# The gate-weight tile and the compressed-probability step of a sparse-attention layer, moved

## The chip, the cores and the metric

The kernel runs on one core of a Trainium2 chip. The metric is the device time of one execution in microseconds (us). A core has five engines with a queue each: PE (matrix multiply), DVE (vector), ACT (scalar functions and copies), POOL (general) and SP, which here only starts DMAs. Each queue is worked off in order; engines wait for each other through semaphores. PE writes into PSUM, and the others move data from there to SBUF, the on-chip memory from which PE reads. PE's weight loads stand apart in the profile as PEld.

## The reference, cut to what matters

Two layers over 256 positions of width 1024: the first with latent attention, the second with sparse attention, each followed by a layer of looked-up experts (PEER). The change lies in the second layer's attention. Each of 16 heads (4 groups of 4) sees three branches: compressed blocks of 32 keys, selected blocks, and a window. At this size the last two reduce to causal attention over all positions, with keys and values of their own. The three results are added with gates that are sigmoids of a projection.

```python
proj = x @ w_in
q = proj[..., :B_HEADS * B_DK]
q_rot = rope(q)
gates = jax.nn.sigmoid(proj[..., B_HEADS * B_DK:])
...
p_c = masked_softmax(qb . k_cmp * scale, cmp_end <= t)
o_c = p_c . v_cmp
...
p_s = masked_softmax(qrb . k_g * scale, tok <= t)
o_s = p_s . v_g
...
p_w = masked_softmax(qrb . k_w * scale, m_w)
o_w = p_w . v_w
return gate0 * o_c + gate1 * o_s + gate2 * o_w
```

## The kernel before

All weights come as one stream of 512 KB tiles, in the order of the list in `plan()`. SP loads a tile into one of four raw places; ACT casts it to `hi` (L173), and a vector engine writes the rest to `lo` (L187); PE multiplies hi and lo parts of weights and activations (L267), three products for each. A raw place comes free when the tile four ahead has its `lo`. `nxt()` hands out the next tile: it emits the casts of the tiles two or three ahead, and then calls `tick()`. A tick counts up and runs what `defer(n, f)` put off for n ticks. So the order of each engine's queue is the order in which Python emits, and a tile that is moved moves the ticks with it.

In `nsa()` the order of work before is:

- Four tiles `s_wT` give the keys and values to be compressed (`kk`). POOL adds position vectors to them (`fm`).
- One tile `b_wg` holds the gate weights (48 of 128 columns are used). Its projection goes through ACT's sigmoid (L1495) to `gs`.
- Four more tiles `s_wT` give the keys of the two rotated branches, two tiles each. `rope_T` (L1345) multiplies on DVE (`ropeU`, `ropeV`) and combines on POOL (`ropeO`). It turns the layout through memory: a DMA writes `bounce`, and another reads it into `kr`. For the first branch both DMAs go through SP, a tick and two ticks later; for the second through POOL, at once. Five ticks later `k_split` splits `kr` with three ACT operations and a DVE one (L1510 to L1513) into `ks` and `klo`. After the second branch PE transposes `gs` (L294), and DVE copies it to `gates` (L1508).
- Eight tiles `b_wq` give the queries. A group of four heads takes two tiles, and each group goes through `rope_T` and `q_split` (L1524, L1525) to `qs`. The unrotated query is copied by ACT to `qu` (L1550). Between the first four query tiles stand four steps of `compress`, which multiply `fm` with the first layer of the compression network. Its hidden values `hb` go through ACT's Gelu, its second layer to the compressed keys `kcp` and values `vcp`.
- A loop of 19 steps over the heads. In step st PE makes the scores of head st (`ks`, `klo` with `qs`), DVE their maxima `m` (L1692, L1693), and ACT the exponentials `p` (L1716, L1719). DVE, or DVE and POOL, normalises `p` of head st-1 with the gates (L1729). PE transposes `p` of head st-2, ACT copies it to `pT` (L1710), and every second step PE sums the values of a pair of heads. The compressed branch goes in two halves of eight heads beside it: `cmp_scores` (`kcp` with `qu`, DVE L1634), `cmp_exp`, `cmp_sum` (POOL L1651) and `cmp_T`. The last has PE transpose `pc` (L294) and ACT copy it to `pcT` (L1657). For the first half these stand at the ends of steps 1, 2, 3 and 4, for the second at 5, 6, 7 and 9.

The ACT functions sigmoid, Gelu and exponential need tables; `ACT_TABLE_LOAD` changes them, and `warm()` (L307) changes them ahead of use with a small activation.

Of the kernel before, what the change touches and what calls it, by code (L numbers as in the profile page):

```python
# [18 lines left out]
AF = mybir.ActivationFunctionType  # L19
# [28 lines left out]
class Kern:  # L48
# [5 lines left out]
    def plan(self):  # L54
# [10 lines left out]
        for l in (0, 1):  # L65
            if l == 1 and "nsa" in self.parts:
                L += [I["s_wv"][i] for i in range(4)]
                L += [I["s_wT"][i] for i in range(4)]
                L += [I["b_wg"]]
                L += [I["s_wT"][i] for i in range(4, 8)]  # L70
                L += [I["b_wq"][i] for i in range(4)]
                L += [I["b_wq"][i] for i in range(4, 8)]
                L += [I["b_wo"][i] for i in range(KC)] + [I["b_wo"][i] for i in range(KC // 2)]
# [1332 lines left out]
    def nsa(self, hN, gb):  # L1406
# [4 lines left out]
        with es:  # L1411
# [79 lines left out]
            hi, lo = self.nxt()  # L1491
            gp = self.ps()
            self.proj_T(gp[:, 0:S], hi, lo, xhi, xlo, KC)
            gs = tmp.tile([48, S], F32, tag="gs", name="gs", bufs=1)
            nc.scalar.activation(gs, gp[0:48, 0:S], AF.Sigmoid)  # L1495

            for br in range(2):
# [6 lines left out]
                if br == 1:  # L1504
                    gt = self.ps()
                    for tt in range(2):
                        self.tr(gt[:, tt * 48:tt * 48 + 48], gs[:, tt * P:(tt + 1) * P])
                    nc.vector.tensor_copy(gates, gt[:, 0:96].rearrange("p (a b) -> p a b", a=2))  # L1508
# [60 lines left out]
            self.warm(AF.Gelu)  # L1569
            hp = self.acc(1)  # L1570
            turn = [0, 0]
            self.vlim = self.si + 7
            for step in "qqcc", "qc", "qc":
                for x in step:
                    if x == "q":
# [93 lines left out]
            for half, when in ((0, (1, 2, 3, 4)), (1, (5, 6, 7, 9))):  # L1669
# [3 lines left out]
            for st in range(NH + 3):  # L1673
# [49 lines left out]
                if 0 <= h < NH:  # L1723
# [3 lines left out]
                    for br, eng in ((1, nc.gpsimd if 4 <= h < NH - 2 else nc.vector), (0, nc.vector)):  # L1727
                        for tt, c in enumerate((slice(0, P), slice(P, 384))):
                            eng.tensor_scalar(p[:, br, c], p[:, br, c], m[:, 3, 2 * tt + br:2 * tt + br + 1],  # L1729
                                              gates[:, tt, 16 * br + 16 + h:16 * br + 17 + h], op0=OP.mult, op1=OP.mult)  # L1730
                h = next((h for h in range(1, NH, 2) if h + (4 if h < 6 else 3) == st), None)
                if h is not None:
# [4 lines left out]
                    for e in range(2):  # L1737
                        self.mm(o[e], vcp[:, hb, (h - 1 + e) % 8, :], pcT[:, hb, :], True, False)
                    for br in range(2):
                        c = br * 256 + g * 64  # L1740
                        for e in range(2):
                            self.mm(o[e], vN[:, 0, c:c + 64], pp[e][:, br, 0:S], False, False)
                        for e in range(2):
                            self.mm(o[e][:, P:S], vN[:, 1, c:c + 64], pp[e][:, br, S:384], False, br == 1)
# [114 lines left out]
```

## Time and profile before

| | before |
|---|---|
| median of 3 runs | 1579.82 us (1579.65 to 1583.05) |
| the profiled execution | 1585.52 us |
| its span, first to last instruction | 1583.5 us |
| matmul clock granted, mean | 0.996 of full |
| stage of the change: first compressed tile to the end of the head loop | about 782 to 907 us of the span |
| PE busy, 800 to 814 | 14.00 of 14 us |
| PE busy, 814 to 830 | 13.93 of 16 us |
| PE busy, 830 to 855 | 21.82 of 25 us |
| DVE busy, 830 to 855 | 22.56 of 25 us |
| PE busy, 880 to 906 | 25.50 of 26 us |

A time in a row of the timeline is counted from the start of the span. Busy times are of one execution. PE's matmuls are pipelined and their ends are modelled, so its starts are more reliable than its ends. A row names the engine, the line, the operation, what is written and what is read, the shapes and a count; in brackets stands the idle time ahead of it and what ended it.

### The profile page before, as it was taken

To read this page: it belongs to the slowest core of one execution; us is meant where nothing else is said; L and a number is where in the kernel's file an instruction comes from. 1 tells how busy PE (TensorE), PEld (TensorE's weight loads), DVE (VectorE), ACT (ScalarE), POOL (GpSimd) and SP (SyncE) were. 2 spreads that over 40 slices of the span, in tenths; PEclk is the share of its full clock that TensorE was granted. 3 is DMA by queue.
4 is the path that set the end of the run, shared out by engine and by line. 5 is a ranking of instruction groups with operands and counts; after the bars stand their busy time and mean duration, and the time that the engine had idled before them with its cause. 6 is when DMAs were issued, how large, how long until landed. Compare 5 with 4: busy or idle time off the path is not lost.

```text
span 1583.5 us, 27544 instructions
## 1 busy us (share of the span) xinstructions
PE 1551.1 (98%) x10018; PEld 1395.6 (88%) x10018; DVE 1387.3 (88%) x3218; ACT 680.8 (43%) x1351; POOL 535.3 (34%) x458
## 2 busy tenths in 40 slices
PE   7999999999999999999998999999999999999997
PEld 6879999999998888888887789999999988888886
DVE  5778889999969999999778789899999869999998
ACT  6665201212225555556367854111121245555553
POOL 2010134443325434431353210344443436434420
PEclk9999999999999999999999999999999999999999
DMA  7626899999999999999564257999999999999992
GB/s 240 202 84 225 330 409 408 408 408 371 396 381 371 373 366 347 357 368 322 187 228 149 79 195 279 408 409 408 408 407 362 371 372 406 353 368 344 360 356 92
DMA packets 140215, 511.03 MB, mean 323 GB/s; under 512 B 14160, under 2 KB 16752, under 8 KB 138992
## 3 DMA queue, kind: packets, MB, share of 16 engines
q1 hardware_dynamic: 89712, 324.70, 55.2%
q0 software_dynamic: 50368, 184.57, 30.6%
q8 instruction: 79, 1.29, 0.3%
q14 instruction: 56, 0.46, 0.1%
HBM read 503.45 MB, written 5.24 MB: 321 GB/s over the span
## 4 chain that ended last, share of the span: by engine, by line
PE 77%; DVE 11%; DMA 8%; ACT 2%; issue 2%; POOL 1%; SPq 0%; ACTq 0%; POOLq 0%; DVEq 0%
PE acc L267 44%; PE mm L267 32%; DMA row<-p_ur,xidx 4%; DVE row L584 3%; DMA nat<-p_u 1%; PE mm L294 1%; DVE lo L187 1%; DMA raw<-a_wv 1%; DVE hot L765 1%; DVE hot L776 1%; DMA raw<-s_wT 1%; DMA xT<-xT 1%; ACT hi L173 1%; DMA kr<-bounce 0%; DVE p L1729 0%
## 5 line engine op out<-in xcount | busy, mean ns | idle before, releaser
L267 PE MATMUL acc<-hi,W 128*128 128x512 f32 x1452 | 408.0, 389 | 0.0
L571 POOL DMA_INDIRECT row<-p_v,gidx x128 | 237.3, 1854 | 311.4 <-DVE gacc L608 243.8
L267 PE MATMUL mm<-xF,nat 128*128 128x160 f32 x2304 | 322.9, 300 | 1.4 <-DMA nat<-p_u 1.3
L267 PEld LDWEIGHTS acc<-hi,W 128*128 128x128 f32 x1452 | 272.5, 188 | 56.4
L267 PEld LDWEIGHTS mm<-xF,nat 128*128 128x128 f32 x2304 | 314.6, 190 | 2.7 <-issue 2.2
L267 PE MATMUL acc<-lo,W 128*128 128x512 f32 x968 | 298.1, 389 | 0.0
L187 DVE TENSOR_TENSOR lo<-raw,hi 128x1024 fp32r<-128x1024 f32 (+1 forms) x202 | 245.2, 1220 | 45.0 <-ACT hi L173 32.5
L173 ACT CAST hi<-raw 128x1024 fp32r<-128x1024 f32 (+1 forms) x207 | 215.1, 1046 | 153.1 <-PE acc L267 110.8
L571 POOL DMA_INDIRECT row<-p_ur,gidx x128 | 140.3, 1096 | 267.6 <-DVE row L584 167.1
L267 PEld LDWEIGHTS acc<-lo,W 128*128 128x128 f32 x968 | 181.8, 188 | 37.7
L173 ACT CAST hi<-spare 128x1024 fp32r<-128x1024 f32 x122 | 128.2, 1051 | 109.0 <-PE acc L267 107.1
L584 DVE SCALAR_TENSOR_TENSOR row<-row,gacc 128x1024 f32<-128x1024 f32 x128 | 155.6, 1218 | 6.5 <-DMA row<-p_ur,gidx 5.8
L608 DVE SCALAR_TENSOR_TENSOR gacc<-row,ggate,gacc 128x1024 f32<-128x1024 f32 x126 | 160.9, 1277 | 0.0
L187 DVE TENSOR_TENSOR lo<-spare,hi 128x1024 fp32r<-128x1024 f32 x122 | 148.7, 1218 | 10.7 <-ACT hi L173 10.7
L267 PE MATMUL mm<-xF,raw 128*128 128x160 f32 x896 | 125.8, 300 | 0.0
L267 PE MATMUL mm<-xF,more 128*128 128x160 f32 x896 | 125.7, 300 | 0.0
L267 PEld LDWEIGHTS mm<-xF,more 128*128 128x128 f32 x896 | 122.6, 190 | 0.0
L267 PEld LDWEIGHTS mm<-xF,raw 128*128 128x128 f32 x896 | 122.6, 190 | 0.0
L801 ACT ACTIVATE A<-acc 128x208 f32<-128x208 f32 (+19 forms) x116 | 37.4, 346 | 190.1 <-DVE A L799 163.4
L891 ACT ACTIVATE A<-mm 128x320 f32<-128x320 f32 (+13 forms) x104 | 38.3, 368 | 176.7 <-PE mm L267 175.0
L911 DVE TENSOR_TENSOR W<-A,W 128x128 fp32r<-128x128 f32 (+1 forms) x512 | 106.9, 249 | 0.0
L571 POOL DMA_INDIRECT row<-p_ur,xidx x64 | 66.0, 1032 | 104.6 <-DVE row L584 43.9
(308 smaller groups left out, 2074.5 us busy)
## 6 DMA issues: line engine op xcount, KB each, us to landing
nat<-p_u SPq DMA_DIRECT2D x144, 512.0 KB, 8.7
spare<-p_v SPq DMA_DIRECT2D x64, 1024.0 KB, 9.0
raw<-p_v SPq DMA_DIRECT2D x63, 1024.0 KB, 8.6
raw<-p_u SPq DMA_DIRECT2D x56, 512.0 KB, 16.3
more<-p_u SPq DMA_DIRECT2D x56, 512.0 KB, 18.3
raw<-p_wq SPq DMA_DIRECT2D x32, 512.0 KB, 4.3
raw<-b_wo SPq DMA_DIRECT2D x12, 512.0 KB, 4.1
raw<-a_wo SPq DMA_DIRECT2D x8, 512.0 KB, 3.5
```

Source lines behind the costliest of these rows:

```text
L173: self.nc.scalar.copy(self.his[i], self.raws[i])
L187: e.tensor_tensor(self.los[i], raw, self.his[i].bitcast(F32), op=OP.subtract)
L267: self.nc.tensor.matmul(out, a, b, start=start, stop=stop)
L294: self.nc.tensor.transpose(out, in_, self.ident[:n, :n])
L571: nc.gpsimd.indirect_dma_start(out=t, out_offset=None, in_=table, in_offset=bass.IndirectOffsetOnAxis(ap=at, axis=0))
L584: nc.vector.scalar_tensor_tensor(t, t, 1.0, x, op0=OP.mult, op1=OP.mult, accum_out=d[:, c:c + 1])
L608: nc.vector.scalar_tensor_tensor(gacc, t, ggate[:, c:c + 1], gacc, op0=OP.mult, op1=OP.add)
L765: tt(h[:, 0:2].rearrange("p w g i s -> p (w g) i s"), self.iota4[:, 0, None].to_broadcast([P, 4, P, 2]), selI[:, t0 // 4].rearrange("p w ( ...
L776: tt(o, oj, x[:, :, None, :].to_broadcast(b4), op=OP.mult)
L801: nc.scalar.activation(x[:, m:n, t0:t0 + 4], pv[:, j0 + m:j0 + n], AF.Copy, scale=sc_)
L891: nc.scalar.activation(y[:, :, n:NU], ps[:, :, n:NU], AF.Gelu)
L911: nc.vector.tensor_tensor(WW[j][:, o:o + c.stop - c.start], slot(j)[:, c], WW[j][:, c].bitcast(F32), op=OP.subtract)
```

## The change

Three things are moved; no arithmetic is added or removed.

1. In the stream the tile `b_wg` goes from ahead of the last four `s_wT` tiles to behind the first two query tiles. Its projection and the sigmoid become `gate_tile()`, the transposes of `gs` and the copy to `gates` become `gate_T()`, and the hand-written order of query tiles (q) and compress steps (c) becomes q q g c c t, q c, q c. The switch to the Gelu table moves into `gate_tile()`. The limit `vlim` on early loads counts one tile more, because one more tile is still to come.
2. The transposes of the first half's `pc` go from the end of step 4 into step 5, behind the transposes of `p`.
3. In the sums of all pairs of heads, the two matmuls with `pcT` go from first to last.

```diff
--- before.py
+++ after.py
@@ -66,10 +66,10 @@
             if l == 1 and "nsa" in self.parts:
                 L += [I["s_wv"][i] for i in range(4)]
                 L += [I["s_wT"][i] for i in range(4)]
+                L += [I["s_wT"][i] for i in range(4, 8)]
+                L += [I["b_wq"][i] for i in range(2)]
                 L += [I["b_wg"]]
-                L += [I["s_wT"][i] for i in range(4, 8)]
-                L += [I["b_wq"][i] for i in range(4)]
-                L += [I["b_wq"][i] for i in range(4, 8)]
+                L += [I["b_wq"][i] for i in range(2, 8)]
                 L += [I["b_wo"][i] for i in range(KC)] + [I["b_wo"][i] for i in range(KC // 2)]
             if f"peer{l}" in self.parts:
                 L += [I["p_wq"][l, i] for i in range(16)]
@@ -1488,11 +1488,20 @@
                     nc.gpsimd.tensor_tensor(f[:, 8:16, g, :], b, posT[:, i, 8:16, None].to_broadcast([P, 8, 15]), op=OP.add)
                 fm.append(f)
 
-            hi, lo = self.nxt()
-            gp = self.ps()
-            self.proj_T(gp[:, 0:S], hi, lo, xhi, xlo, KC)
             gs = tmp.tile([48, S], F32, tag="gs", name="gs", bufs=1)
-            nc.scalar.activation(gs, gp[0:48, 0:S], AF.Sigmoid)
+
+            def gate_tile():
+                hi, lo = self.nxt()
+                gp = self.ps()
+                self.proj_T(gp[:, 0:S], hi, lo, xhi, xlo, KC)
+                nc.scalar.activation(gs, gp[0:48, 0:S], AF.Sigmoid)
+                self.warm(AF.Gelu)
+
+            def gate_T():
+                gt = self.ps()
+                for tt in range(2):
+                    self.tr(gt[:, tt * 48:tt * 48 + 48], gs[:, tt * P:(tt + 1) * P])
+                nc.vector.tensor_copy(gates, gt[:, 0:96].rearrange("p (a b) -> p a b", a=2))
 
             for br in range(2):
                 ps = self.ps()
@@ -1501,11 +1510,6 @@
                     self.proj_T(ps[:, hf * S:(hf + 1) * S], hi, lo, xhi, xlo, KC)
                 kr = tmp.tile([64, G, S], F32, tag="raw4", name="kr")
                 self.rope_T(tmp, ps.rearrange("p (a t) -> p a t", a=2), rK, kr, 1, 2, br == 1)
-                if br == 1:
-                    gt = self.ps()
-                    for tt in range(2):
-                        self.tr(gt[:, tt * 48:tt * 48 + 48], gs[:, tt * P:(tt + 1) * P])
-                    nc.vector.tensor_copy(gates, gt[:, 0:96].rearrange("p (a b) -> p a b", a=2))
                 def k_split(br=br, kr=kr):
                     nc.scalar.copy(ks[0:64, :, br, :], kr)
                     nc.vector.tensor_tensor(klo[0:64, :, br, :], kr, ks[0:64, :, br, :].bitcast(F32), op=OP.subtract)
@@ -1566,12 +1570,14 @@
                                 w1[q][:, i, m % 4, :], m == 0, m == 15)
 
 
-            self.warm(AF.Gelu)
             hp = self.acc(1)
             turn = [0, 0]
-            self.vlim = self.si + 7
-            for step in "qqcc", "qc", "qc":
+            self.vlim = self.si + 8
+            for step in "qqgcct", "qc", "qc":
                 for x in step:
+                    if x in "gt":
+                        (gate_tile if x == "g" else gate_T)()
+                        continue
                     if x == "q":
                         q_tile(turn[0])
                         turn[0] += 1
@@ -1666,7 +1672,7 @@
                      4: ((7, 1), (7, 2))}
             beside = {2 * k + (7 if k < 3 else 6): lambda k=k: self.out_step(k) for k in range(KC - 2)}
             cmp_at = {}
-            for half, when in ((0, (1, 2, 3, 4)), (1, (5, 6, 7, 9))):
+            for half, when in ((0, (1, 2, 3, None)), (1, (5, 6, 7, 9))):
                 for w, f in zip(when, (cmp_scores, cmp_exp, cmp_sum, cmp_T)):
                     cmp_at[w] = lambda f=f, half=half: f(half)
             pr, pts = {}, {}
@@ -1728,20 +1734,22 @@
                         for tt, c in enumerate((slice(0, P), slice(P, 384))):
                             eng.tensor_scalar(p[:, br, c], p[:, br, c], m[:, 3, 2 * tt + br:2 * tt + br + 1],
                                               gates[:, tt, 16 * br + 16 + h:16 * br + 17 + h], op0=OP.mult, op1=OP.mult)
+                if st == 5:
+                    cmp_T(0)
                 h = next((h for h in range(1, NH, 2) if h + (4 if h < 6 else 3) == st), None)
                 if h is not None:
                     pvp = self.ps()
                     pp = [pts.pop(h - 1), pts.pop(h)]
                     hb, g = h // 8, h // HG
                     o = [pvp[64 * e:64 * e + 64, 0:S] for e in range(2)]
-                    for e in range(2):
-                        self.mm(o[e], vcp[:, hb, (h - 1 + e) % 8, :], pcT[:, hb, :], True, False)
                     for br in range(2):
                         c = br * 256 + g * 64
                         for e in range(2):
-                            self.mm(o[e], vN[:, 0, c:c + 64], pp[e][:, br, 0:S], False, False)
+                            self.mm(o[e], vN[:, 0, c:c + 64], pp[e][:, br, 0:S], br == 0, False)
                         for e in range(2):
-                            self.mm(o[e][:, P:S], vN[:, 1, c:c + 64], pp[e][:, br, S:384], False, br == 1)
+                            self.mm(o[e][:, P:S], vN[:, 1, c:c + 64], pp[e][:, br, S:384], False, False)
+                    for e in range(2):
+                        self.mm(o[e], vcp[:, hb, (h - 1 + e) % 8, :], pcT[:, hb, :], False, True)
                 for i, x in parts.get(st, ()):
                     if x == 2:
                         q_after(i)
```

ACT's queue around the gates, before (hi is the cast of a weight tile, gs the sigmoid, wsq the small activation behind a table change, ks and klo the keys):

```order
L173 CAST hi<-raw 128x1024
L1495 ACT_TABLE_LOAD
L1495 ACTIVATE gs<-mm 48x256
L173 CAST hi<-raw 128x1024 x4
L307 ACT_TABLE_LOAD
L307 ACTIVATE wsq<-lneps 128x1
L173 CAST hi<-raw 128x1024 x2
L1550 COPY qu<-acc 128x512
L1510 CAST ks<-kr 64x4x256
L1512 CAST ks<-ks 64x4x256
L1513 CAST klo<-klo 64x4x256
```

The same place in the change:

```order
L173 CAST hi<-raw 128x1024 x6
L1554 COPY qu<-acc 128x512
L173 CAST hi<-raw 128x1024
L1514 CAST ks<-kr 64x4x256
L1516 CAST ks<-ks 64x4x256
L1517 CAST klo<-klo 64x4x256
L1497 ACT_TABLE_LOAD
L1497 ACTIVATE gs<-mm 48x256
L307 ACT_TABLE_LOAD
L307 ACTIVATE wsq<-lneps 128x1
L1514 CAST ks<-kr 64x4x256
```

The sigmoid and the Gelu table now stand behind the first branch's three key casts and ahead of the second branch's.

PE's queue at the gates, as a difference (mm<-hT is a key tile or the gate tile, acc<-hT a query tile, w and fm a compress step):

```order
-L267 MATMUL mm<-hT,hi 128x256 x16
-L267 MATMUL mm<-hT,lo 128x256 x8
-L294 MATMUL mm<-ident,gs 128x48 x2
 L267 MATMUL acc<-hT,hi 128x256 x16
 L267 MATMUL acc<-hT,lo 128x256 x8
 L267 MATMUL acc<-hT,hi 128x256 x16
 L267 MATMUL acc<-hT,lo 128x256 x8
+L267 MATMUL mm<-hT,hi 128x256 x16
+L267 MATMUL mm<-hT,lo 128x256 x8
 L267 MATMUL acc<-w_7382,fm_7483 60x256
```

One tile of the gates' form now follows the first two query tiles. The transposes of gs follow two compress steps later, directly ahead of the third query tile:

```order
 L267 MATMUL acc<-w_7399,fm_7483 60x256
 L267 MATMUL acc<-w_7399,fm_7562 60x256
+L294 MATMUL mm<-ident,gs 128x48 x2
 L267 MATMUL acc<-hT,hi 128x256 x16
 L267 MATMUL acc<-hT,lo 128x256 x8
```

PE's queue in step 5 of the head loop, as a difference, from the transposes of p on:

```order
 L294 MATMUL mm<-ident,p 128x128 x6
-L267 MATMUL mm<-pcT,vcp 64x256 x2
+L294 MATMUL acc<-ident,pc 128x128 x2
 L267 MATMUL mm<-pT,vN 64x256 x2
 L267 MATMUL mm<-pT,vN 64x128 x2
 L267 MATMUL mm<-pT,vN 64x256 x2
 L267 MATMUL mm<-pT,vN 64x128 x2
+L267 MATMUL mm<-pcT,vcp 64x256 x2
```

The pc transposes, which were the last of step 4, now come in step 5, and the pcT matmuls end the sum.

ACT's queue at the same place, in the change (qu is the copy that ends step 4, p the exponentials of step 5, pcT the copy of the pc transposes); before, pcT stood between qu and qs:

```order
L1554 COPY qu<-acc 128x512
L1528 CAST qs<-qr 64x512 x2
L1716 COPY pT<-mm 128x384 x2
L1722 ACTIVATE p,m<-mm,m 128x128 x2
L1725 ACTIVATE p,m<-acc,m 128x256 x2
L1663 COPY pcT<-acc 128x256
L283 CAST oT<-mm 128x256
```

The copy to pcT now stands behind four exponentials.

## The prediction

> **What bounds the kernel now.** I read the page first, then the waits of PE, then the timeline of the stretches that the change touches.
>
> ```profile
> span 1583.5 us, 27544 instructions
> ...
> PE 1551.1 (98%) x10018; PEld 1395.6 (88%) x10018; DVE 1387.3 (88%) x3218; ACT 680.8 (43%) x1351; POOL 535.3 (34%) x458
> ```
>
> PE is busy for 98% of the span, so a change can only gain where PE starves or runs slowly, and it loses wherever it makes PE starve anew. The waits of PE (who it waited for, the sum in us, times, the longest) name such places; in the changed stage these are the two large ones:
>
> ```profile
> PE acc L294 <- POOL pc L1651: 3.2, 1, 3.2
> PE mm L267 <- DVE qs L1525: 2.1, 1, 2.1
> ```
>
> PE waits 3.2 us for the compressed probabilities pc and 2.1 us for qs, the first query group. Together with what the first of them does to the clock (below), these are all that the change can win.
>
> The sum is made against the profiled execution (1585.52 us, its span 1583.5), which is 5.7 us above the median of the runs shown (1579.82). The differences worked out here are then added to the median.
>
> **Part one, the gate tile.** On PE nothing is added or removed: 24 matmuls and two transposes move. The first column is the start, then comes the duration; the bracket is the idle time before it.
>
> ```profile
> 808.32 0.32 PE L294 MATMUL mm<-ident,gs 48*128 48x48 f32 x2
> ...
> 814.23 3.67 PE L267 MATMUL acc<-w,fm 128*60 128x256 f32 x32
> ...
> 825.66 1.94 PE L267 MATMUL acc<-gb,fm 128*60 128x256 f32 x16
> 829.67 0.36 PE L267 MATMUL mm<-ks,qs 128*128 128x256 f32 x1 [2.07 <-DVE qs L1525]
> ```
>
> Before, the transposes of the gates (808.32) met no wait. PE ran on to 827.60 and then starved for 2.07 us until qs. In the change PE reaches the end of the first two compress steps (817.90 here) 0.25 us earlier, since the two transposes are no longer ahead of it (808.32 to about 808.57, when the next tile began). So PE wants the gates at 817.65. What stands in front of them now is on ACT: the cast of the next query tile, the three casts of the first rotated keys (ks, ks, klo), then the table load and the sigmoid gs. So I follow those keys.
>
> ```profile
> 800.31 2.62 DVE L187 TENSOR_TENSOR lo<-raw,hi 128x1024 fp32r<-128x1024 f32 x2
> ...
> 804.70 0.69 DVE L1350 TENSOR_TENSOR ropeU<-mm,pcT 128x512 f32<-128x512 f32 x1
> ...
> 806.08 1.64 POOL L1353 TENSOR_TENSOR ropeO<-ropeU,ropeV 128x256 f32<-128x256 f32 x1 [2.32 <-DVE ropeV L1351]
> ...
> 807.69 1.71 POOL L1354 TENSOR_TENSOR ropeO<-ropeU,ropeV 128x256 f32<-128x256 f32 x1
> ...
> 809.42 0.38 SPq L1357 DMA_DIRECT2D bounce<-ropeO  x1
> ...
> 813.88 0.52 SPq L1360 DMA_DIRECT2D kr<-bounce  x1
> ```
>
> The rope of the first key branch comes behind two lo subtractions in the change, not three. These two end at 802.93. From the start of ropeU to POOL's start were 1.38 (804.70 to 806.08), so POOL starts at 804.31, 1.77 earlier than here. Its two halves take 3.32 beside DVE's subtractions, as here. Everything behind moves by those 1.77: the bounce is written from 807.65, kr is read from 812.1, and the keys have landed at about 816.35 (their cast began at 818.13, directly on the DMA, below). On SP the bounce write and the kr read each pass one weight load. Those loads are a tile ahead of their use, which hides them, and I cost them at nothing; without that cover a cast is late by up to the 3.93 us that the wait at 810.62 shows. POOL's queue keeps its order.
>
> ```profile
> 800.79 1.28 ACT L1495 ACT_TABLE_LOAD   x1
> 802.09 0.38 ACT L1495 ACTIVATE gs<-mm 48x256 f32<-48x256 f32 x1
> ...
> 810.62 1.05 ACT L173 CAST hi<-raw 128x1024 fp32r<-128x1024 f32 x1 [3.93 <-DMA raw<-b_wq]
> ...
> 818.13 1.05 ACT L1510 CAST ks<-kr 64x1024 fp32r<-64x1024 f32 x1 [0.87 <-DMA kr<-bounce]
> ...
> 820.46 1.04 ACT L1513 CAST klo<-klo 64x1024 fp32r<-64x1024 f32 x1 [0.21 <-DVE klo L1511]
> 822.90 1.05 ACT L1510 CAST ks<-kr 64x1024 fp32r<-64x1024 f32 x1 [1.39 <-DMA kr<-bounce]
> ```
>
> From the start of ks to the end of klo are 3.37 us (818.13 to 821.50). The table load and gs take 1.68 (800.79 to 802.47); before, they stood there, where PE had other work. So gs is ready at 816.35 + 3.37 + 1.68 = 821.4, and PE, there at 817.65, waits **3.75 us for the gates**. ACT sets nearly the same limit without that DMA: behind the cast that ended its wait for b_wq at 811.67 come a lo (1.31, half of the 2.62), the rope (1.38), qu (0.59, a row below) and a cast (1.05), which gives 816.0 for ks.
>
> Behind the waiting transposes on PE is all the rest of the stage: the next two query tiles, the last two compress steps and the first scores. The matmuls among them took 9.70 us (817.90 to 827.60). So the scores begin at 821.4 + 0.25 + 9.7 = 831.35 instead of 829.67. Is qs late by then? After gs comes the second table load (1.28), and then the casts of the second keys, which start at about 822.7, as at 822.90 here. From there to the scores were 6.77 us, so qs is ready at about 829.5. The old wait goes, the new one is larger: **+1.7 us**.
>
> Bounds: if that b_wq tile and the keys both landed 2 us sooner, gs would come at 819.4, the wait would be 1.75, and the scores would begin at 829.35: -0.3. If the keys land no earlier than now, at 818.1, it is 5.5 and +3.4. I take +1.7, from the nearest rows. It goes on through the stage, for the chain of the work that ended last runs from PE's matmuls through the keys of the compressed blocks into DVE:
>
> ```profile
> 834.64 1.91 PE acc L267 x17
> ...
> 836.57 0.72 DVE kcp L1600 x2
> ```
>
> **Part two, the clock.** After the times, the rows give PE, PEld, DVE, ACT and POOL busy, and then the granted clock:
>
> ```profile
> 830.00:855.00 25.00, 21.82 (x181) 20.14 (x180) 22.56 (x51) 18.19 (x55) 7.47 (x9) 1.00 0.48 150
> ...
> 856.00:857.00 1.00, 1.00 (x6) 0.92 (x6) 1.00 (x3) 0.03 (x1) 0.00 (x0) 0.51 0.33 131
> ...
> 862.00:863.00 1.00, 1.00 (x8) 1.00 (x6) 0.00 (x0) 0.63 (x3) 0.64 (x2) 0.58 0.67 234
> 863.00:864.00 1.00, 1.00 (x12) 1.00 (x10) 0.00 (x0) 0.00 (x0) 0.00 (x0) 1.00 0.82 270
> ```
>
> After the 3.19 us of idling that ended at 854.70, the clock fell to half at 856.0 and came back at about 862.85. Behind the idle 2.07 us before 829.67 it stayed at 1.00. The new wait of 3.75 lies above the gap that did drop it, so I expect a drop behind it. PE has 9.7 us of unbroken work there, so half speed costs half of its length. That length was 6.85 us here, but PE starved again inside it (0.76 at 858.33, below). Without that I take half of the length, 3.4 us, and so **+1.7 us**. Ends: nothing, as after the 2.07, and +3.4 for the full length.
>
> [...]
>
> **Part three, the compressed probabilities.** The transposes of pc went ahead of step 5's scores and now stand behind its p transposes. So the 3.19 us go, and what is late next is p:
>
> ```profile
> 854.70 0.44 PE L294 MATMUL acc<-ident,pc 128*128 128x128 f32 x2 [3.19 <-POOL pc L1651]
> ...
> 854.93 1.25 DVE L1729 TENSOR_SCALAR p<-p,m,gates 128x128 f32<-128x128 f32 x4
> ...
> 856.01 1.56 PE L294 MATMUL mm<-ident,p 128*128 128x128 f32 x6
> ...
> 857.41 0.59 ACT L1550 COPY qu<-acc 128x512 f32<-128x512 f32 x1 [1.39 <-DVE ropeV L1351]
> ...
> 857.90 0.38 ACT L1657 COPY pcT<-acc 128x256 f32<-128x256 f32 x1
> 858.16 1.14 ACT L1524 CAST qs<-qr 64x512 fp32r<-64x512 f32 x2
> ...
> 858.33 1.12 PE L267 MATMUL mm<-pcT,vcp 128*64 128x256 f32 x4 [0.76 <-ACT pcT L1657]
> ...
> 861.80 0.48 ACT L1719 ACTIVATE p<-acc,m 128x256 f32<-128x256 f32 x1
> ...
> 861.94 2.41 PE L267 MATMUL mm<-kcp,qu 128*128 128x64 f32 x16
> ...
> 864.16 0.36 PE L267 MATMUL mm<-ks,qs 128*128 128x256 f32 x1
> ```
>
> DVE writes p of the fourth head from 854.93 to 856.18, and PE's transposes of it began at 856.01, directly behind. DVE's order is unchanged and nothing it did there waited for the pc transposes. In the change PE does the scores 3.2 us earlier and then waits for the same p until the same 856.0: the gap moves and stays some 3.2 us long, so the clock there is taken as unchanged too.
>
> Behind it, pcT now stands on ACT after the exponentials of step 5. Without pcT ahead of it, the qs pair starts 0.26 earlier (at 857.90), and so do DVE's maxima and the exponentials, which end at 862.02 instead of 862.28. pcT takes 0.38, and PE sees it 0.05 later (857.90 + 0.38 against 858.33): 862.45. The matmuls with vN are done by then (858.33 to 861.94 covers them at half speed with the four on pcT), so PE **starves again, for pcT**. The sum now ends with four matmuls on pcT, whose time at full clock these rows give (the next group starts 0.48 behind):
>
> ```profile
> 869.45 0.65 PE L267 MATMUL mm<-pcT,vcp 128*64 128x256 f32 x4
> ...
> 869.93 1.47 PE L267 MATMUL mm<-pT,vN 128*64 128x256 f32 x16
> ```
>
> The second half's scores (kcp with qu) then begin at 862.93, against 861.94 here. At full clock they take 1.71:
>
> ```profile
> 838.31 1.90 PE L267 MATMUL acc<-kcp,qu 128*128 128x64 f32 x16
> ...
> 840.02 0.37 PE L267 MATMUL mm<-ks,qs 128*128 128x256 f32 x1
> ```
>
> So step 6 begins at 864.65, against 864.16: **+0.5 us**. The other end: had the old execution kept its clock, pcT at 858.33 with 0.48, then 1.47 and 1.71 give 862.0, and the new one is 2.7 later. Below nothing it does not go, since ACT's order alone gives 862.45. I take +0.5, because it is measured against the execution whose rows I use. For the later heads pcT is there long before, and the same matmuls in another order cost nothing.
>
> **The sum.** 1.7 + 1.7 + 0.5 = +3.9 us: 1589.4 for an execution like the profiled one, 1583.7 on the median.
>
> **The rivals.**
> (1) The new wait comes, but the clock holds behind it. For it: the gap of 2.07 left the clock alone. Against it: 3.19 did not. +2.2, 1582.0.
> (2) Faster: both waits go as meant. Mechanism: gs is ready when PE reaches 817.65, because the keys have landed by 812.6, 5.5 us earlier than now, and at step 5 PE keeps enough work that the clock stays up and pcT comes no later. Price: -2.07, and step 6 at 862.45 or so instead of 864.16, -1.7: -3.8, 1576.0. Against it: the rope alone moves by only 1.77, and p and the exponentials hold PE at 856.0 and 862.45 whatever the clock.
> (3) The gates come in time, step 5 is late: -2.07 + 0.5 = -1.6, 1578.2. It decides at the same point, gs before 817.65.
>
> **How the numbers follow.** A measurement of this kernel can tell about 0.2% from no change, 3.2 us. Forecast 0.47 (slower), rival 1 0.26 (within), rival 2 0.13 (faster), rival 3 0.14 (within). This makes slower 0.47, same 0.40, faster 0.13. The range leaves out rival 2 and the last few per cent above. It begins at 1577.5, below rival 3. It ends where the full clock loss and the other end of step 5 come with the wait (1.7 + 3.4 + 2.7 = 7.8), a little within that: 1587.3.
>
> **What would show it.** In the profile of the changed kernel: a wait of the gate transposes for ACT's gs of 2.5 to 4.5 us, with the casts of kr, the table load and gs in one row on ACT ahead of it; no wait for qs at the first scores; the granted clock near 0.5 for some 3.4 us behind the gates; in step 5 a wait for DVE's p of about 3 us and one for pcT. The prediction is wrong if the keys' casts end before PE has finished the second compress step, or if the wait for p in step 5 is much shorter than the wait for pc was.

## The result, and the profile after

The changed kernel took 1594.29 us (median of 4 runs, 1591.2 to 1595.26) beside 1581.43 us for the kernel before (median of 4, 1579.65 to 1585.34): a ratio of 1.0069, 95% interval 1.0049 to 1.0088. The two medians lie 12.9 us apart; the ratio, by which "some 11 us" is meant below, puts it at 10.9, with 8 to 14 in its interval. 3.9 us slower was forecast; 1594.29 lies above the range (1577.5 to 1587.3).

The page of the changed kernel (its profiled execution took 1591.2 us, with a mean granted clock of 0.993 against 0.996):

```profile
span 1589.2 us, 27543 instructions
...
PE 1553.3 (98%) x10018; PEld 1398.4 (88%) x10018; DVE 1387.0 (87%) x3218; ACT 680.6 (43%) x1351; POOL 542.1 (34%) x458
```

PE does the same 10018 matmuls and is busy for 2.2 us longer; the span is 5.7 us longer. The waits of PE between 780 and 890 us, whom it waited for, sum, times, longest:

```profile
PE mm L294 <- DVE p L1735: 3.7, 2, 3.6
PE mm L294 <- ACT gs L1497: 3.7, 1, 3.7
PE mm L267 <- ACT pcT L1663: 2.8, 1, 2.8
```

The waits for pc (3.2) and qs (2.1) are gone, as the change wanted. In their place stand three: for p, for the gates and for pcT. The timeline of PE around the gates (start, duration, and in brackets the idle time before, and what ended it):

```profile
812.84 3.67 PE L267 MATMUL acc<-w,fm 128*60 128x256 f32 x32
820.23 0.32 PE L294 MATMUL mm<-ident,gs 48*128 48x48 f32 x2 [3.71 <-ACT gs L1497]
820.48 2.70 PE L267 MATMUL acc<-hT,hi 128*128 128x256 f32 x16
...
831.64 0.39 PE L267 MATMUL mm<-ks,qs 128*128 128x256 f32 x1
```

And ACT at the same place:

```profile
815.11 1.04 ACT L1514 CAST ks<-kr 64x1024 fp32r<-64x1024 f32 x1 [0.83 <-DMA kr<-bounce]
...
818.50 1.28 ACT L1497 ACT_TABLE_LOAD   x1
819.80 0.38 ACT L1497 ACTIVATE gs<-mm 48x256 f32<-48x256 f32 x1
```

The key casts, the table load and gs stand in one row, and PE starves behind them for 3.71 us. The timeline of PE, and behind it that of ACT, in step 5:

```profile
857.99 0.99 PE L294 MATMUL mm<-ident,p 128*128 128x128 f32 x6 [3.56 <-DVE p L1735]
...
859.13 2.69 PE L267 MATMUL mm<-pT,vN 128*64 128x256 f32 x16
864.58 1.12 PE L267 MATMUL mm<-pcT,vcp 128*64 128x256 f32 x4 [2.77 <-ACT pcT L1663]
865.63 3.68 PE L267 MATMUL mm<-kcp,qu 128*128 128x64 f32 x16
869.07 0.56 PE L267 MATMUL mm<-ks,qs 128*128 128x256 f32 x1
```

```profile
863.70 0.48 ACT L1725 ACTIVATE p<-acc,m 128x256 f32<-128x256 f32 x1
...
864.15 0.38 ACT L1663 COPY pcT<-acc 128x256 f32<-128x256 f32 x1
```

PE waits for p, runs its 16 matmuls with vN, and starves again until ACT has done the last exponential of step 5 and pcT. The scores with kcp then take 3.44 us (865.63 to 869.07). The first half's took 1.71 at full clock, and the second half's take 1.80 in the kernels below whose clock is full there.

In the changed stage of this execution the granted clock falls at 821.78 and 859.32 and rises at 825.19 and 872.97. The shortest time between two of these edges is 3.41 us, and the others are 10 and 4 times as long (34.13 and 13.65), to 0.03 us. So the windows below are cut on that grid. Each row has the window, its length and how long PE was busy in it, then the busy times of PEld, DVE, ACT and POOL, the granted clock, and two figures on DMA. What is missing from PE's busy time to the length is PE's idling:

```profile
814.95:818.36 3.41, 1.56 (x16) 0.72 (x12) 1.22 (x1) 3.00 (x3) 1.42 (x2) 1.00 1.04 366
818.36:821.78 3.42, 1.55 (x13) 1.50 (x14) 0.00 (x0) 3.36 (x6) 0.00 (x0) 1.00 0.59 167
821.78:825.19 3.41, 3.41 (x17) 3.09 (x18) 2.52 (x3) 3.14 (x4) 0.53 (x1) 0.50 0.28 73
855.91:859.32 3.41, 1.33 (x10) 1.08 (x12) 3.37 (x9) 1.72 (x8) 0.62 (x1) 1.00 0.65 225
859.32:862.73 3.41, 2.50 (x16) 1.39 (x13) 2.21 (x5) 2.55 (x6) 2.48 (x4) 0.50 0.26 77
862.73:866.15 3.42, 1.57 (x7) 0.81 (x7) 1.07 (x4) 2.17 (x10) 1.18 (x2) 0.50 0.61 248
866.15:869.56 3.41, 3.41 (x17) 3.41 (x17) 0.21 (x1) 0.00 (x0) 0.00 (x0) 0.50 0.47 138
869.56:872.97 3.41, 3.41 (x15) 2.83 (x14) 2.74 (x8) 0.98 (x3) 1.31 (x3) 0.50 0.00 0
872.97:876.39 3.42, 3.42 (x26) 2.50 (x27) 2.76 (x6) 3.42 (x12) 1.94 (x3) 1.00 0.00 0
```

One window at half follows the gates, four in a row (13.65 us) follow the wait for p. Before, cut on its own grid, it was two (6.83 us):

```profile
852.60:856.01 3.41, 1.31 (x9) 0.86 (x9) 3.27 (x12) 2.16 (x10) 0.62 (x1) 1.00 0.89 271
856.01:859.42 3.41, 2.65 (x13) 1.79 (x14) 1.98 (x4) 2.02 (x6) 1.96 (x4) 0.50 0.09 36
859.42:862.84 3.42, 3.42 (x22) 2.33 (x19) 2.46 (x7) 2.61 (x11) 1.70 (x3) 0.50 0.65 222
```

To compare executions, times below are counted from the stage's first matmul with the compressed tiles (782.26 before, 781.66 after).

| from the stage's first matmul, us | before | after | difference |
|---|---|---|---|
| to the first scores | 47.41 | 49.98 | +2.57 |
| first scores to the scores of step 6 | 34.49 | 37.43 | +2.94 |
| step 6 to the matmuls behind the head loop | 42.44 | 44.22 | +1.78 |
| sum | 124.34 | 131.63 | +7.29 |

The third row grew because the slow stretch reaches 3.9 us into step 6 (869.07 to 872.97). A smaller share of it, 0.3 us, is the order of the sums: three kernels below with pcT last and full clock there (step 5 with pcT sooner, both mended, the wait for pcT filled) have 42.76 in this row.

### The profile page after: what moved, and what is told of

It reads as the page before. It is cut to its first block, busy times and chain, and to the rows that moved or that the text cites. A ratio compares the mean times of both kernels' runs of the same rounds, so it can differ in the third digit from the quotient of the medians.

```text
span 1589.2 us, 27543 instructions
## 1 busy us (share of the span) xinstructions
PE 1553.3 (98%) x10018; PEld 1398.4 (88%) x10018; DVE 1387.0 (87%) x3218; ACT 680.6 (43%) x1351; POOL 542.1 (34%) x458
## 4 chain that ended last, share of the span: by engine, by line
PE 78%; DVE 12%; DMA 6%; ACT 2%; issue 1%; POOL 1%; SPq 0%; ACTq 0%; POOLq 0%; DVEq 0%
PE acc L267 45%; PE mm L267 32%; DVE row L584 3%; DMA row<-p_ur,xidx 3%; DMA nat<-p_u 1%; PE mm L294 1%; DMA bounce<-ropeO 1%; DVE lo L187 1%; DVE hot L776 1%; DMA raw<-s_wT 1%; DVE hot L765 0%; ACT hi L173 0%; DMA raw<-p_wq 0%; DVE idx L647 0%; DVE p L1735 0%
## 5 line engine op out<-in xcount | busy, mean ns | idle before, releaser
L571 POOL DMA_INDIRECT row<-p_v,gidx x128 | 244.8, 1913 | 303.7 <-DVE gacc L608 235.9
```

What stands on the lines that cost most here:

```text
L571: nc.gpsimd.indirect_dma_start(out=t, out_offset=None, in_=table, in_offset=bass.IndirectOffsetOnAxis(ap=at, axis=0))
```

## The experiments

Twelve runs were made, each beside the kernel before on the same chip. "Half" is the time at half clock in the stage, and "stage" the sum of the table above, both of the one profiled execution; the clock is the mean over all runs of the kernel. The ratio is to the runs of before on the same chip, not to the 1583.5 of all of them.

| kernel | median us | ratio to before (95%) | clock | half | stage |
|---|---|---|---|---|---|
| before | 1583.5 (104 runs) | | 0.9962 | 6.8 | 124.3 |
| change, again | 1595.31 | 1.0074 (1.0053 to 1.0094) | 0.9928 | 17.1 | 132.9 |
| gate tile alone | 1587.16 | 1.0024 (1.0011 to 1.0037) | 0.9946 | 10.2 | 126.6 |
| step 5 alone | 1589.27 | 1.0032 (1.0019 to 1.0046) | 0.9933 | 17.1 | 129.9 |
| change, PE kept awake | 1588.89 | 1.0039 (1.0025 to 1.0053) | 0.9970 | 0 | 128.3 |
| before, PE kept awake | 1583.3 | 0.9997 (0.9984 to 1.001) | 0.9974 | 3.4 | 124.1 |
| gate tile, gs first | 1583.39 | 1.0002 (0.9989 to 1.0014) | 0.9966 | 0 | 121.6 |
| step 5, pcT sooner | 1582.76 | 0.9999 (0.9986 to 1.0011) | 0.9967 | 0 | 124.0 |
| both mended | 1582.29 | 1.0001 (0.9993 to 1.001) | 0.9966 | 6.8 | 124.4 |
| change, pcT wait filled | 1589.79 | 1.0035 (1.0022 to 1.0049) | 0.9954 | 3.4 | 125.9 |
| change, p wait filled | 1594.2 | 1.0059 (1.004 to 1.0078) | 0.9933 | 13.7 | 133.4 |
| pc before, pcT early | 1582.68 | 0.9993 (0.9979 to 1.0006) | 0.9969 | 3.4 | 122.3 |
| that with gs first | 1583.22 | 1.0006 (0.9991 to 1.002) | 0.9967 | 3.4 | 122.2 |

### The change again

The same kernel once more.

> The changed kernel once more, for the spread of its runs beside those of before on one chip. Theory W: 7 to 11 us above before, lowest runs where only the two half-speed stretches of the first profile occur, higher ones with a lower mean clock.

Measured: 1595.31 us, 1.0074. The loss stands. In this execution the gates cost 4.7 us of waiting and 6.8 us at half clock, so what happens at the gates differs from one execution to the next. In step 5 the slow time came in two pieces:

```profile
856.30:859.71 3.41, 0.60 (x4) 0.51 (x5) 3.29 (x11) 1.72 (x8) 0.62 (x1) 1.00 0.72 280
859.71:863.12 3.41, 3.41 (x20) 2.33 (x20) 2.25 (x4) 2.37 (x5) 2.48 (x4) 0.50 0.08 28
863.12:866.54 3.42, 1.12 (x11) 0.48 (x9) 1.77 (x5) 2.12 (x10) 1.18 (x2) 1.00 0.81 260
866.54:869.95 3.41, 3.41 (x18) 3.41 (x18) 0.16 (x1) 0.23 (x1) 0.00 (x0) 0.50 0.57 181
```

Behind the wait for p comes one window at half, then one at full clock. Into that one falls the wait for pcT (2.30 us), and the clock goes down again, for two windows (866.54 to 873.36).

### One part alone

Gate tile alone: the diff of the change without its last three hunks.

> Only the gate tile is moved; the compressed probabilities stay as before. Theory W (each new wait costs its length plus the half-speed stretch behind it): the gate transposes wait 3.7 us for gs, no wait for qs, half clock for about 3.4 us behind; first scores 50 us behind the first compressed-key matmul against 47.4 before; median +2.5 to +4 us (about 1583 to 1585). Step 5 as before. Rival S (the gate move carries most of the loss): median +8 us or more.

Step 5 alone: only these hunks of the change.

```diff
-            for half, when in ((0, (1, 2, 3, 4)), (1, (5, 6, 7, 9))):
+            for half, when in ((0, (1, 2, 3, None)), (1, (5, 6, 7, 9))):
...
+                if st == 5:
+                    cmp_T(0)
...
-                    for e in range(2):
-                        self.mm(o[e], vcp[:, hb, (h - 1 + e) % 8, :], pcT[:, hb, :], True, False)
...
+                    for e in range(2):
+                        self.mm(o[e], vcp[:, hb, (h - 1 + e) % 8, :], pcT[:, hb, :], False, True)
```

> Only the compressed probabilities are moved (transposes in step 5, last in the sums); the gate tile stays as before. Theory W: the waits for p (3.6 us) and for pcT (2.8 us) stand close together, the clock stays at half from the first to some 8 us after the second, 10 to 14 us in all; median +6 to +9 us (1586 to 1589), the larger part of the change's loss. Rival S (pcT is a late guest only): +0.5 to +1 us, as the prediction's step had it.

Measured: 1.0024 (3.8 us, as expected) and 1.0032 (5.1 us, less than the 6 to 9 expected, though the slow time, 17.1 us in one stretch, was longer than the 10 to 14). Both parts lose on their own, and the two together (0.56%) come near the whole (0.69 and 0.74%, within their intervals). Step 5, for which 0.5 us was forecast, has the larger median; the two intervals overlap, so which is larger is not shown.

### Where the loss is clock and where it is waiting

The change with spare transposes of the identity on PE, which nothing reads: 30 ahead of the gate transposes, 28 behind step 5's scores and 20 ahead of step 5's sum. At full clock the 28 took 3.22 us and the 20 took 2.35; at that pace 30 take some 3.5, as an estimate. That is less than the waits in which they stand (3.71, 3.56 and 2.77 us in the change).

```diff
                 gt = self.ps()
+                for _ in range(30):
+                    self.tr(gt[:, 128:256], self.ident)
...
+                if st == 5:
+                    early.append(self.acc(0))
+                    for _ in range(28):
+                        self.tr(early[0][:, 256:384], self.ident)
...
+                    if st == 5:
+                        for _ in range(20):
+                            self.tr(pvp[:, 256:384], self.ident)
```

> The whole change, with identity transposes on PE inside the three waits (30 ahead of the gate transposes, 28 ahead of step 5's p transposes, 20 ahead of its sum), whose results nobody reads. The waits for data last as long as before, but PE is busy in them. Theory W: the granted clock stays at 1.00 in the stage, and the median is 1583 to 1586, 8 to 11 us below the change's 1594. Rival L (the loss is the waiting itself): no more than 3 us below the change.

And the same for the wait for pc in the kernel before:

```diff
                 tp = self.acc(0) if hb == 0 else self.ps()
+                for _ in range(27 if hb == 0 else 0):
+                    self.tr(tp[:, 256:384], self.ident)
```

> The kernel before, with 27 identity transposes on PE ahead of the transposes of pc in step 4, inside the 3.2 us wait. Theory W: the clock stays at 1.00 in step 5, step 6 begins some 2 us earlier than in the profile of before, the runs cluster at or a little below the lower runs of before (1578 to 1580), without those at 1583 to 1585. Rival L: same as before, with the same spread.

Measured: with PE kept awake the change takes 1588.89 us, its stage has no time at half clock, and 0.8, 0.5 and 1.8 us of waiting are left behind the three groups of spare work. Both expectations missed: 1583 to 1586 was expected if the loss were nearly all clock, 1591 or more if it were the waiting. Some 5.5 of its 11 us (1588.89 against 1583.4, the median of before beside it) remain at full clock, and about as much was the clock. The granted clocks say the same: the change's mean over 10 runs is 0.9925, before's over 104 is 0.9962, and 0.0037 of 1590 us are 5.9 us. Before, the same trick gains nothing that can be told (0.9997), where 1578 to 1580 was expected: in the profiled execution of that kernel the wait for qs had 3.8 us, and brought the clock down instead.

### Mending ScalarE's order

Gate tile alone, with the gates' table load and gs ahead of the first branch's key casts. One tick is enough:

```diff
-                self.defer(5, k_split)
+                self.defer(6 - br, k_split)
```

> The gate tile moved as in the change, the compressed probabilities as before, and the key split of the first branch put off by one tick, so that on ACT the table loads and the sigmoid stand ahead of its casts. Theory W (PE waits for gs because ACT stands at the first branch's keys): the wait of the gate transposes falls from 4 to 5 us to under 0.5, no half-speed stretch there, qs is waited for by some 1 us again, the first scores come 1 to 2 us earlier than before, counted from the stage's first matmul (47.4 before, 49.8 with the gate tile alone). Median 3 to 6 us below the gate tile alone, 0 to 2 below the kernel before. Rival (gs is late because its own projection or table load is late): the wait stays above 2 us and the time that of the gate tile alone.

Step 5 alone, with its cmp_T(0) right behind the transposes of p, so that pcT stands ahead of the four exponentials on ACT; PE's order is the change's:

```diff
                     pts[h] = pT
+                if st == 5:
+                    cmp_T(0)
                 h = st
                 if h < NH:
                     p = prob.tile([P, 2, 384], F32, tag="p", name="p")
```

> Only the compressed probabilities moved, but the pc transposes and the copy to pcT emitted right behind step 5's p transposes, so that on ACT the copy stands ahead of the four exponentials; PE's order is the change's. Theory W (pcT is late because it stands behind the exponentials, and that second wait keeps the clock down): the wait for pcT falls by about 2 us, the scores of the second half (kcp with qu) start 79.0 to 80.0 us behind the stage's first matmul (81.85 with the copy behind the exponentials, 79.7 before), the half-speed stretch is at most that of before (6.8 us). Median 3 to 5 us below that other version, within 2 of the kernel before. Rival (the move of the transposes itself, with the wait for p, costs it): still 4 us or more above before.

Both moves with both orders mended:

> Both moves of the change, each with its order on ScalarE mended: the gates' copies stand ahead of the first branch's key casts, and pcT stands ahead of step 5's four exponentials (TensorE's order in step 5 is the change's). If the change's whole loss is the two places on ScalarE and the slow clock that follows them, nothing of it is left: within 3 us of the kernel before, no gate wait over 1 us, no pcT wait over 2 us. The two mended halves gained 2.8 us (gates) and 0.4 us (pcT) in the stage, counted from its first matmul to the output projection, in one profiled execution each; if they add, some 3 us faster than before in the stage, and what lies around it unchanged. Rival: moving the gate tile and the pc transposes costs something in itself, beside those waits: then it stays 4 us or more slower than before.

Measured: 1.0002, 0.9999 and, for both, 1.0001 (0.9993 to 1.001). The whole loss is gone, and no gain can be told. With gs first, ACT and then PE in their timelines:

```profile
815.87 1.28 ACT L1497 ACT_TABLE_LOAD   x1
817.17 0.38 ACT L1497 ACTIVATE gs<-mm 48x256 f32<-48x256 f32 x1
...
818.97 1.03 ACT L1514 CAST ks<-kr 64x1024 fp32r<-64x1024 f32 x1
```

```profile
817.60 0.32 PE L294 MATMUL mm<-ident,gs 48*128 48x48 f32 x2 [0.32 <-ACT gs L1497]
...
829.13 0.36 PE L267 MATMUL mm<-ks,qs 128*128 128x256 f32 x1 [1.49 <-DVE qs L1529]
```

The gates come in time, and the wait for qs is back. With pcT sooner, PE in step 5 of that kernel:

```profile
855.00 1.00 PE L294 MATMUL mm<-ident,p 128*128 128x128 f32 x6 [3.56 <-DVE p L1731]
...
859.09 0.65 PE L267 MATMUL mm<-pcT,vcp 128*64 128x256 f32 x4 [1.43 <-ACT pcT L1657]
```

The wait for p is as long as in the change (3.56), the one for pcT is 1.43 us. It was 2.77 in the change and 1.85 with step 5 alone, both at half clock, where the sum ahead of it takes longer (2.69 us for its 16 matmuls in the change, 1.52 at full clock with PE kept awake); at full clock it is 3.94 in a kernel further below. A fall by 2 us was expected. With both mended PE waits 1.2 us for the gates, a little over the expected 1, and not at all for pcT. The wait for p does bring the clock down there, but only for one window:

```profile
852.10:855.51 3.41, 0.00 (x0) 0.00 (x0) 3.27 (x12) 2.17 (x10) 0.62 (x1) 1.00 0.72 247
855.51:858.92 3.41, 3.29 (x18) 2.53 (x20) 2.24 (x4) 2.03 (x6) 1.83 (x3) 0.50 0.15 60
858.92:862.34 3.42, 3.42 (x32) 2.64 (x29) 2.50 (x7) 2.74 (x12) 1.83 (x4) 1.00 0.77 232
```

So the cause of the loss is shown: on ACT, the casts ahead of the gates and the exponentials ahead of pcT. The rival, that moving the gate tile or the pc transposes costs 4 us or more in itself, is out. The hope of 3 us of gain rested on stage times of executions in which the clock happened not to drop (0 us at half, against 6.8 before).

### Which wait holds the clock down

The change with 11 spare transposes ahead of step 5's sum, so that the wait for pcT alone is filled:

```diff
                     o = [pvp[64 * e:64 * e + 64, 0:S] for e in range(2)]
+                    if st == 5:
+                        for _ in range(11):
+                            self.tr(pvp[:, 256:384], self.ident)
```

> The change with 11 spare transposes of the identity on TensorE ahead of step 5's sum, so that only the wait for pcT is filled (11 of them take 1.3 us at full clock and 2.5 us at half); the waits for the gates and for p stay. [...] The wait for p brings the clock down, and idling inside the slow stretch (the wait for pcT) is what keeps it down for 13.65 us. With that wait filled the slow stretch of step 5 is one or two windows, 3.4 to 6.8 us, and the time falls by 2 to 4 us: ratio to the kernel before some 1.0045 to 1.006. Rival: the wait for p and the short matmuls behind it keep the clock down whatever happens in between: still 10 us or more at half in step 5, and a time like the change's (1.007).

The change with the 28 behind step 5's scores alone:

> The change with 28 spare transposes of the identity (3.2 us) behind step 5's scores, so that only the wait for p is filled; the waits for the gates and for pcT stay. Theory: no drop behind p. The wait for pcT is then met at full clock, where the sum ahead of it ends sooner, so it is longer, some 3.5 to 4 us, and brings the clock down itself for one or two windows (3.4 to 6.8 us), over the scores with kcp. Time 2 to 4 us under the change's: ratio to the kernel before 1.0045 to 1.006. Rival: the long slow stretch comes from the wait for p alone: then no drop in step 5 at all, and the time is 4 to 6 us under the change's (ratio 1.003 to 1.0045).

Measured: filling the wait for pcT brings 1.0074 down to 1.0035, a little more than expected, and its interval (1.0022 to 1.0049) leaves out the rival's 1.007. The windows of that execution, cut on its grid:

```profile
814.55:817.97 3.42, 1.63 (x16) 0.79 (x12) 1.22 (x1) 3.16 (x4) 0.83 (x2) 1.00 0.98 290
817.97:821.38 3.41, 2.19 (x19) 2.14 (x20) 0.00 (x0) 3.37 (x5) 0.00 (x0) 1.00 0.64 180
852.10:855.51 3.41, 0.02 (x1) 0.05 (x1) 3.27 (x12) 2.17 (x10) 0.62 (x1) 1.00 0.84 275
855.51:858.93 3.42, 3.42 (x16) 3.33 (x17) 2.25 (x5) 2.04 (x6) 1.99 (x4) 0.50 0.08 32
858.93:862.34 3.41, 2.22 (x23) 1.46 (x23) 2.35 (x6) 2.32 (x10) 1.69 (x3) 1.00 0.82 253
```

Behind the wait for p comes one window at half, in which PE is never idle, and the clock is back. At the gates PE starved for 3.01 us here, and the clock held: the wait was split between two windows, 1.79 and 1.22 of idling. Filling the wait for p alone (1.0059) leaves most of the loss. The drop behind p is gone, but at full clock the wait for pcT grows to 3.94 us and makes a drop of its own:

```profile
861.17:864.59 3.42, 2.06 (x22) 1.36 (x20) 2.24 (x4) 2.37 (x5) 2.49 (x4) 1.00 0.10 32
864.59:868.00 3.41, 0.83 (x6) 0.45 (x7) 1.77 (x5) 2.12 (x10) 1.18 (x2) 1.00 0.90 250
868.00:871.41 3.41, 3.41 (x18) 3.41 (x18) 0.15 (x1) 0.24 (x1) 0.00 (x0) 0.50 0.68 192
871.41:874.83 3.42, 3.42 (x15) 2.84 (x15) 2.79 (x8) 0.93 (x3) 1.26 (x2) 0.50 0.00 0
```

The rival, that the wait for p alone makes the long slow stretch, falls with these windows; the time alone would not decide, since its interval reaches down to 1.004 and the rival had 1.003 to 1.0045. It is the wait for pcT that holds the clock down in the change (13.65 us at half in step 5, 3.41 with that wait filled), or brings it down anew (6.83 us in the change again), and that can do so alone (6.83 us here).

### Another order, as a candidate

The kernel before with the scores of step 5 emitted at the end of step 4, ahead of the pc transposes, so that PE has work while POOL finishes pc, and pcT stands ahead of qu on ACT:

```diff
+            sc = []
+
+            def scores(h):
...
+                    s0v, s1v = sc.pop() if sc else scores(h)
...
+                if st == 4:
+                    sc.append(scores(5))
+                    cmp_T(0)
                 for i, x in parts.get(st, ()):
```

Here `scores(h)` holds the six matmuls that make the scores of head h.

> The kernel before with one other order: the scores of step 5 go ahead of the pc transposes on PE, and the copy to pcT goes ahead of the last query copy qu on ACT, at the end of step 4; pcT stays first in the sums. Theory W: the wait for pc shrinks from 3.2 to about 2 us, a second short wait for p of about 1 us follows, pcT is there before PE wants it, and kcp with qu starts 77.5 to 78.5 us behind the stage's first matmul (79.7 before). Median 1 to 3 us below before. Rival (DVE's p bounds all of it): same as before within 0.5 us.

The same with the gate tile moved and gs first:

> The gate tile moved with its copies early on ScalarE, and in place of the change's second part the scores of step 5 ahead of the pc transposes, which stay in step 4. Of the stage, the first half gained 2.8 us and the second 2.1 us in one profiled execution each. If both are real and add: 3 to 5 us faster than the kernel before (ratio 0.997 to 0.998). If the gains in the profiled executions were only the clock that happened not to drop there: no difference that can be told, within 2 us.

Measured: 0.9993 (0.9979 to 1.0006) and 1.0006 (0.9991 to 1.002). Neither differs from before in a way that can be told. The waits came as expected for the first (2.3 us for pc, 0.9 for p, and kcp with qu at 78.0), the 1 to 3 us of gain did not. The stages of the profiled executions were 2 us shorter, with 3.4 us less at half clock, but the medians don't show it; that those gains were only the clock of one execution fits this and is not shown further.

## Why the prediction was right in its direction and wrong in its size

**The gates: right.** 3.75 us of waiting were forecast and 3.71 came, with ACT's order as the cause (gs first takes it away). That it fits to 0.04 us is luck: in the five profiled executions with this order the wait was 3.0, 3.7, 4.2, 4.7 and 4.8 us, and counted from the stage's first matmul PE and gs came 0.5 and 0.6 us earlier than forecast. The wait for qs went, as forecast. Behind the gates one window at half was forecast, and one came: the work from the transposes to the scores took 11.16 us (820.48 to 831.64) instead of 9.70. Wait and clock together were forecast at +3.4 up to the first scores; +2.57 was measured, and +4.47 in the second profiled execution of the change (51.88 against 47.41). Rival 1, that the clock holds behind the gates, happens too: the execution with the wait for pcT filled shows it. There the wait lay as 1.79 and 1.22 us of idling in two windows, in the change as 1.85 and 1.87. The two rows that the prediction set against each other differ in the same way: before, the 2.07 us for qs that left the clock alone lay across two windows (1.09 and 0.98 of idling), and most of the 3.19 us that dropped it lay in one (2.10).

**Step 5's waits: right.** "The gap moves and stays some 3.2 us long" came as 3.56 us for p, and "starves again, for pcT" as 2.77 us. The order of ACT behind it is as forecast: with pcT sooner the wait is 1.43 us, with both mended there is none.

**The step that failed** is the end of part three: "so the clock there is taken as unchanged too", and with it the +0.5. The clock was half for 13.65 us instead of 6.83 (10.2 in the second execution). The sum counted the second wait as time, but not as idling inside a slow stretch. The clock stayed at half in the window of that wait (862.73 to 866.15, 1.85 us of idling) and in two more behind it, and so for the four matmuls on pcT (1.05 us instead of 0.48), the scores with kcp (3.44 instead of 1.71) and 3.9 us of step 6. Part two had a row for this: it named the 0.76 us of starving at 858.33 as what had stretched the slow time before to 6.85 us, but part three, which put a new wait at the same place, did not use it. Measured from the first scores on, the term is +2.94 and +1.78, 4.7 us in all, beyond the other end that was given for it (2.7), because that end had the new execution at full clock behind pcT. With that one wait filled by 11 transposes, the same kernel gets half of its loss back (1.0074 to 1.0035). One part stays open: the last of the four slow windows follows one in which PE was never idle (866.15 to 869.56).

**A small miss beside it:** "the same matmuls in another order cost nothing" holds but for 0.3 us, as the third row of the table shows.

**The base was low.** 3.9 us were added to 1579.82, the median of three runs. Over 104 runs the kernel before has a median of 1583.5. The profiled execution, set aside as 5.7 us above the median, was 2.0 above that one. On the better base the range would have ended at 1591.0, still below 1594.29, so the base is not the whole of the miss.

**What stays open.** The two stages differ by 7.3 us in the profiled pair and the spans by 5.7, while the medians differ by 10.9 to 12.9. Both profiled executions of the change (1591.2, 1591.63) are among the fastest of its runs, and before's (1585.52) is one of its slower ones. The runs of the change that took 1594 us and more had granted clocks of 0.991 to 0.993, so more windows at half are likely in some, but none of those has a trace.

**The chances.** Slower had 0.47 and came. The direction rested on the gates, and that part held. The range's upper end did put the wait for the gates, a longer slow stretch behind them and the other end of step 5 together (7.8 us); no case had a longer slow stretch in step 5.

## What to carry to other kernels

When an instruction is moved, look at what stands ahead of its producer on the producer's own engine: here both new waits of PE were made by ACT's order, and two moves in the order of emission took away the whole loss (1.0001). Where a trace shows the edges of the clock on a grid, as these do (3.41 us), count PE's idling by its windows and not gap by gap alone, and price a wait inside a slow stretch by the work behind it that may run at half clock, as the scores with kcp did here (3.44 us instead of 1.71). A dozen spare matmuls in the wait show what it costs (11 brought 1.0074 down to 1.0035). A base taken from three runs of a kernel that scatters by 10 us can be off by as much as the change.

## What the runs showed of the hardware

In 12 of the 14 profiled executions the stretch from about 785 to 887 us was cut into windows of 3.41 us, on a grid through one edge of the clock in that execution. The granted clock of each window is 0.99 to 1.00 or 0.50 to 0.51, so no edge in these stretches lies off its grid by more than some 0.1 us. 348 of the windows have another behind them. Of those at full clock, all 17 in which PE idled for 1.87 to 3.41 us were followed by one at half (the one with 1.87, 818.36 to 821.78 in the change, was busy for 1.55 of its 3.42 us); none of the 18 with 1.01 to 1.85 us was, nor any of the 283 with less. All 9 windows at half with 0.55 to 1.85 us of idling were followed by another at half; of the 21 with 0.19 us or less 17 were followed by full clock. The other 4 (866.15 to 869.56 above is one, 868.00 to 871.41 another) are just those in which the scores with kcp, matmuls of 64 columns, take 1.6 us or more. These are counts of this kernel's executions; why the clock does so is not shown. The two other executions, the change kept awake and the gate tile with gs first, have no edge in the stage; PE's longest waits there are 1.75 and 3.18 us, and how those fall on a grid is not shown.

So a gap of one length went either way here. In the change the 3.56 us for p put 2.08 us of idling into the window 855.91 to 859.32, and the clock fell behind it. With pcT sooner a gap of 3.56 us was split into 1.85 and 1.71, and the clock held, as these windows of that kernel show:

```profile
849.88:853.29 3.41, 1.56 (x12) 1.01 (x10) 3.31 (x8) 2.19 (x4) 0.27 (x1) 1.00 0.29 106
853.29:856.70 3.41, 1.70 (x14) 1.29 (x16) 3.05 (x8) 2.01 (x9) 0.60 (x2) 1.00 0.57 207
```
